# Seven block products for gate and up in both feed-forward layers, activation forms summed by accumulating DMAs, and weight loads issued by a plan of times

## The chip, the core and the metric

The kernel runs on one core of a Trainium2 chip. TensorE (PE) multiplies, with its weight loads shown as an engine of their own (PEld); VectorE (DVE), ScalarE (ACT) and GpSimd (POOL) do the element work; SyncE (SP) issues most DMAs, GpSimd some. Every engine runs its own instructions in order and waits for others by semaphores, and so does each engine that issues DMAs. The metric is the device time of one execution in microseconds (us), the median of the runs.

## The reference, cut to what matters

A decoder trunk of two layers over 512 tokens and width 1024. Layer 0 mixes by a recurrent group (RG-LRU) and a stick-breaking attention group, layer 1 by sliding-window attention (SWA); each is followed by a conv-gated MLP with 2816 inner channels. Six vectors per layer (shift, scale and gate, twice) come from `c` by one large matrix, `ada_w`.

```python
def adaln_params(c, w, b):
    m = jax.nn.silu(c) @ w + b
    return [t[:, None, :] for t in jnp.split(m, 6, axis=-1)]

def conv_ffn(h, w_gate, w_up, conv_w, conv_b, w_down):
    a = causal_dwconv(h @ w_gate, conv_w, conv_b)
    return (jax.nn.silu(a) * (h @ w_up)) @ w_down

for layer in range(DEPTH):                       # 2
    sh1, sc1, g1, sh2, sc2, g2 = adaln_params(c, ada_w[layer], ada_b[layer])
    h = rms_norm(x, norm_mix_g[layer]) * (1.0 + sc1) + sh1
    mix = ...                                    # RG-LRU + stick-breaking, or SWA
    x = x + g1 * mix
    h = rms_norm(x, norm_ffn_g[layer]) * (1.0 + sc2) + sh2
    x = x + g2 * conv_ffn(h, ...)
```

## The kernel before

**Numbers.** Every float32 operand of a large product is split in two float32r parts, hi (a copy on ACT, L200 or L169) and lo (the difference, on DVE, L201 or L170). A product is three matmuls, hi·hi, hi·lo, lo·hi (`mm3`, L209 to L212). x and h lie as [128, 8 blocks of channels, 512 tokens].

**Feed-forward, layer 0** (`ffn`, L705). For each of 22 blocks `f` of 128 inner channels, gate (`g`) and up (`u`) are each 8 x 3 = 24 matmuls with 512 columns. After groups of 8, 7 and 7 blocks the down products (`d`) of the group follow. Each weight is one load of 512 KB on SP, one hi copy and one lo difference, prepared up to three units ahead (`take`, L188).

**Feed-forward, layer 1** (`ffn_pairs`, L771). Blocks 0 and 1 are done as in layer 0. The other 20 go in ten pairs. For a pair, gate and up weights over the two halves of the channels of h make a 2 x 2 block matrix, h makes another (two halves of channels, two halves of tokens), and the product of the two takes seven block products (slots A to G) and not eight. A slot is 24 matmuls with 256 columns (`product`, L906, matmuls at L917). It needs sums of weight blocks and sums of quarters of h:
- Weights: `s1` and `s3` are loaded by SP and another block is added by an accumulating DMA that POOL issues (L868); `s2` and `s4` are added by POOL (L873, 128x1024).
- h: four forms `n1`, `n2`, `t3`, `t4`. `whole` (L805) puts hi and lo back together on POOL (L811, 8 additions of 128x512); `form` (L815) adds two of these on DVE (L819, L821, 8 operations) and splits the result (L200, L201).
- Slots run in a list `order`: A of pair i, then B, C, D of pair i-1, then E, F, G of pair i; down products after pairs 3 and 7. `upkeep` (L1003) goes ahead of each: loads for the next 9 items, weight sums for the next 4, splits for the next 4. Tile buffers: `raw` 3, `sw` 4, `adaw` 2, split weights 4.

**What goes ahead of a feed-forward.** `out_tail` (L653) ends the mixing layer; `tail` (L630) and `Norm` make h in two halves of tokens. Each of 8 blocks in a half is one DVE operation (L295), one ACT copy to `h` hi (L299) and one DVE operation to `h` lo (L301), all 128x256, while PE runs `g` and `u` of blocks 0 and 1 on what is ready.

**adaLN vectors.** 96 columns; each is a 512 KB load (`adaw`) and one DVE operation of 128x1024 (`ada_col`, L225). 16 are done at the start. `ada_step` (L229) spreads the other 80: 27 of them in the mixing of layer 0 and 53 in the feed-forward of layer 0, three after each block. None stands in layer 1.

**RG-LRU gates.** Two 64-row gate blocks per c are loaded, and split to `gwh` and `gwl` (L504), one buffer each. **SWA** (`swa_s`, L1103): 16 steps, each with sums and maxima (L1124), a reciprocal (L1130) and a scaling (L1132) on DVE, exponentials on ACT (L1128), transposes (L1145) and products on PE; `q`, `out` products go in between.

**Order.** A scheduler orders instructions for each engine by program order and priority; `pin` keeps those named in the order of the program.

## Time and profile before

| | us |
|---|---|
| median of 3 runs | 1152.72 (1151.48 to 1153.03) |
| profiled execution, its own time | 1145.14 |
| span of the profile | 1143.4 |
| PE busy | 1112.9 |
| feed-forward of layer 0, first to last PE instruction | 241.8 to 608.8 |
| feed-forward of layer 1 | 789.6 to 1139.8 |

The span runs from the first to the last instruction. Windows are in us from the span's start. A matmul's duration includes its pipeline, so matmuls overlap; what one costs in a row of many is the length of the stretch over their number.

### The profile page before, as it was taken

Reading aid. Unit: us, or ns where it says so; the run is one execution under the profiler, and the core shown is the slowest. Engines: PE = TensorE matmul, PEld = TensorE weight load, DVE = VectorE, ACT = ScalarE, POOL = GpSimd, SP = SyncE. Lnnn points to the kernel's source line nnn. Section 1 sums busy time; section 2 is a strip of 40 time slices with the busy share of each in tenths; the row PEclk is TensorE's granted clock in tenths of the full one; section 3 lists DMA queues with packets and bytes.
Section 4 is the critical chain, followed back from the end, with each engine's and each line's share of the span. In section 5 each row is a group of like instructions: output and inputs, shape, how many; then the busy total and the mean of one; then the engine's idle time right before and its main releaser. Section 6 shows DMA issues by size and latency. Waiting matters only on the chain.

```text
span 1143.4 us, 16343 instructions
## 1 busy us (share of the span) xinstructions
PE 1112.9 (97%) x6290; PEld 937.4 (82%) x6290; DVE 834.5 (73%) x1283; ACT 535.4 (47%) x864; POOL 111.2 (10%) x99
## 2 busy tenths in 40 slices
PE   8998998999999999999999999999899999999998
PEld 7866776798878888888889766678899889998997
DVE  6975899888873587456557578967999539974873
ACT  4465778354331333223335466644566326641550
POOL 0010000000000000000000111211633102411200
PEclk9999899999999999999999999999999999999999
DMA  9879573625874477445241421035358527573521
GB/s 341 297 188 234 179 213 121 199 69 168 274 225 143 135 225 236 160 148 164 81 143 57 111 57 55 19 93 143 80 136 222 158 77 198 135 236 92 132 72 74
DMA packets 49147, 174.03 MB, mean 152 GB/s; under 512 B 5583, under 2 KB 6735, under 8 KB 48367
## 3 DMA queue, kind: packets, MB, share of 16 engines
q1 hardware_dynamic: 44830, 156.64, 42.9%
q0 software_dynamic: 4240, 16.35, 7.8%
q8 instruction: 49, 0.80, 0.3%
q14 instruction: 28, 0.23, 0.1%
HBM read 164.06 MB, written 2.10 MB: 145 GB/s over the span
## 4 chain that ended last, share of the span: by engine, by line
PE 80%; DVE 9%; DMA 4%; ACT 3%; issue 2%; POOL 1%; SPq 0%; DVEq 0%; ACTq 0%; POOLq 0%
PE y L917 9%; PE d L212 7%; PE d L211 7%; PE d L210 7%; PE x L917 7%; DMA adaw<-adaw 4%; PE g L210 3%; PE g L212 3%; PE g L211 3%; PE u L212 3%; PE u L210 3%; PE u L211 3%; PE o L210 2%; PE o L212 2%; PE o L211 2%
## 5 line engine op out<-in xcount | busy, mean ns | idle before, releaser
L169 ACT ACTIVATE whi_w<-raw_w 128x1024 fp32r<-128x1024 f32 (+1 forms) x113 | 117.8, 1043 | 187.6 <-PE d L211 80.0
L170 DVE TENSOR_TENSOR wlo_w<-raw_w,whi_w 128x1024 fp32r<-128x1024 f32 (+1 forms) x113 | 135.9, 1203 | 46.0 <-ACT whi_w L169 43.5
L225 DVE CUSTOM_DVE_ANT_0 adaw<-adaw,c_s,col 128x1024 f32<-128x1024 f32 x80 | 101.3, 1279 | 35.1 <-DMA adaw<-adaw 34.9
L324 DVE SCALAR_TENSOR_TENSOR x<-d,ada,x 128x512 f32<-128x512 f32 (+1 forms) x51 | 36.6, 719 | 113.9 <-PE d L212 113.9
L211 PE MATMUL g<-h,whi_w 128*128 128x512 f32 (+1 forms) x192 | 72.2, 376 | 3.5 <-DVE h L301 3.5
L210 PE MATMUL g<-h,whi_w 128*128 128x512 f32 (+1 forms) x192 | 72.4, 377 | 1.6 <-ACT h L299 1.4
L212 PE MATMUL u<-h,wlo_w 128*128 128x512 f32 (+1 forms) x192 | 72.1, 376 | 0.0
L210 PE MATMUL d<-ah,whi_w 128*128 128x512 f32 (+1 forms) x190 | 71.9, 378 | 0.2 <-ACT ah L200 0.2
L210 PE MATMUL u<-h,whi_w 128*128 128x512 f32 (+1 forms) x192 | 72.0, 375 | 0.0
L212 PE MATMUL g<-h,wlo_w 128*128 128x512 f32 (+1 forms) x192 | 72.0, 375 | 0.0
L211 PE MATMUL d<-al,whi_w 128*128 128x512 f32 (+1 forms) x190 | 70.8, 373 | 0.8 <-DVE al L201 0.8
L211 PE MATMUL u<-h,whi_w 128*128 128x512 f32 (+1 forms) x192 | 71.5, 372 | 0.0
L212 PE MATMUL d<-ah,wlo_w 128*128 128x512 f32 (+1 forms) x190 | 71.3, 376 | 0.0
L873 POOL TENSOR_TENSOR r_s<-r_s,r_a 128x1024 f32<-128x1024 f32 x20 | 55.1, 2755 | 147.6 <-DVE wlo_s L201 50.2
L200 ACT ACTIVATE whi_s<-r_s 128x1024 fp32r<-128x1024 f32 x40 | 42.5, 1062 | 46.0 <-PE d L211 17.8
L212 PE MATMUL d<-ah,wlo_d 128*128 128x512 f32 (+1 forms) x158 | 60.8, 385 | 0.0
L210 PE MATMUL d<-ah,whi_d 128*128 128x512 f32 (+1 forms) x158 | 60.1, 380 | 0.6 <-DVE x L324 0.6
L211 PE MATMUL d<-al,whi_d 128*128 128x512 f32 (+1 forms) x158 | 60.5, 383 | 0.0
L917 PE MATMUL y<-h,whi_a 128*128 128x256 f32 x320 | 57.1, 280 | 1.0 <-DVE gt L789 1.0
L1121 POOL COPY sc<-nsink 128x4 f32<-128x4 f32 x16 | 3.4, 217 | 560.9 <-PE d L212 502.3
L917 PE MATMUL y<-forms,whi_s 128*128 128x256 f32 x320 | 56.6, 279 | 0.1
L201 DVE TENSOR_TENSOR wlo_s<-r_s,whi_s 128x1024 fp32r<-128x1024 f32 x40 | 51.9, 1297 | 5.6 <-ACT whi_s L200 4.7
(332 smaller groups left out, 3119.8 us busy)
## 6 DMA issues: line engine op xcount, KB each, us to landing
raw_w<-wu SPq DMA_DIRECT2D x104, 512.0 KB, 3.8
adaw<-adaw SPq DMA_DIRECT2D x80, 512.0 KB, 4.4
r_a<-ws SPq DMA_DIRECT2D x30, 512.0 KB, 3.8
r_s<-ws SPq DMA_DIRECT2D x20, 512.0 KB, 4.6
r_s<-ws POOLq DMA_DIRECT2D x20, 512.0 KB, 7.2
first_w<-adaw SPq DMA_DIRECT2D x16, 512.0 KB, 5.7
r_d<-wu SPq DMA_DIRECT2D x16, 512.0 KB, 5.2
raw_w<-w SPq DMA_DIRECT2D x16, 448.0 KB, 3.4
```

The source lines that it names most:

```text
L169: pin(A.activation(hi[:, :n], raw[:, :n], AF.Copy))
L170: pin(V.tensor_tensor(out=lo[:, :n], in0=raw[:, :n], in1=hi[:, :n].bitcast(F32), op=ALU.subtract))
L200: A.activation(dst_hi, src, AF.Copy)
L201: V.tensor_tensor(out=dst_lo, in0=src, in1=dst_hi.bitcast(F32), op=ALU.subtract)
L210: PE.matmul(out, whi, rhi, start=first, stop=False)
L211: PE.matmul(out, whi, rlo, start=False, stop=False)
L212: return PE.matmul(out, wlo, rhi, start=False, stop=last)
L225: return V.tensor_tensor_reduce(out=t, in0=t, in1=c_s, scale=1.0, scalar=C(f"ada_b{l}", s * 8 + m), op0=ALU.mult, op1=ALU.add, accum_out=a ...
L324: V.scalar_tensor_tensor(out=x[:, m, sl], in0=bank[:, sl], scalar=ada_ap(l, s, m), in1=x[:, m, sl], op0=ALU.mult, op1=ALU.add)
L873: G.tensor_tensor(out=self.t, in0=self.base[0].t, in1=self.base[1].t, op=ALU.add)
L917: m = [PE.matmul(out, w[a][:, o:o + P], b[c][:, k], start=slot in "AEF" and k + a + c == 0, stop=k == 3 and a == 1, skip_group_check=True) ...
L1121: nc.gpsimd.tensor_copy(sc[:, :, 256:257], nsink[:, 4 * kv:4 * kv + 4].unsqueeze(2))
```

## The change

1. **Layer 0 uses the seven block products too.** `ffn_pairs` becomes `ffn` for both layers; the old `ffn` goes. The weights of layer 0 are laid out as those of layer 1.
2. **Forms of h.** The 8 POOL additions and 8 DVE additions go. `Norm.chunk` calls `extra`: one more ACT copy of 128x256 per block and half writes the quarters of h in float32, some negated (16 copies a layer). Accumulating DMAs, issued by POOL (`add_to`, ten of 256 KB a layer), add them one after the other into the same tiles; `split_form` splits after each step.
3. **Plan of times.** Each job adds 2.8, 4.1 or 5.5 to a clock. Loads are sorted by use minus `lead` (16, 20, 24 or 26; 8 for adaLN columns) and issued in that order, pinned; `a12` has one buffer of its own. Sums stand 12 ahead of use (accumulating ones `lead` - 5).
4. **adaLN columns.** In the feed-forward of layer 0 41 stand: one in each pair from the third on, two before each down product after pairs 3 and 7, two near the end. Ten go to SWA (one every second step), one to the feed-forward of layer 1.
5. **Gates.** `gwh` and `gwl` become one tile `gw` with two buffers.

```diff
-            gwh = pers.tile([P, 256], F32R, tag="gwh", name=f"gwh{c}", bufs=1)
-            gwl = pers.tile([P, 256], F32R, tag="gwl", name=f"gwl{c}", bufs=1)
+            gw = work.tile([P, 2, 256], F32R, tag="sq", name=f"gw{c}")
+            gwh, gwl = gw[:, 0], gw[:, 1]
...
+        def extra(m, sl, t):
+            if m < 4:
+                A.activation(b["b11"][:, m], t[:, sl], AF.Identity, bias=ada_ap(l, 3, m))
+            else:
+                A.activation(b["n21"][:, m - 4], t[:, sl], AF.Identity, bias=nsh[:, l, m:m + 1], scale=-1.0)
...
+            def extra(m, sl, t):
+                if m < 4:
+                    A.activation(n12[m // 2][:, m % 2], t[:, sl], AF.Identity, bias=nsh[:, l, m:m + 1], scale=-1.0)
+                else:
+                    A.activation(b22[m // 2 - 2][:, m % 2], t[:, sl], AF.Identity, bias=ada_ap(l, 3, m))
...
-            rings = {"raw": (3, []), "sw": (4, []), "adaw": (2, []), "w": (4, [])}
+            rings = {"raw": (3, []), "a12": (1, []), "sw": (4, []), "ada": (4, []), "adaw": (2, []), "w": (4, [])}
...
-                        nc.sync.dma_start(self.t[:, :self.width], self.src)
+                        pin(nc.sync.dma_start(self.t[:, :self.width], self.src))
...
+            def add_to(a, b):
+                for i in range(2):
+                    G.dma_start(a[i], b[i], accum_op=ALU.add)
...
+            def loads(c):
+                now, full = order[c][0].at, set()
+                for it in list(to_load):
+                    if it.at - it.lead > now:
+                        break
+                    if it.t is None and (it.tag in full or not it.room()):
+                        full.add(it.tag)
+                        continue
+                    it.load()
+                    to_load.remove(it)
...
+            loads(0)
+            sums(0, 1)
+            add_to(fb, n12)
+            preps(0, pin)
+            sums(0, 2)
+            for i in ((0, 1), (2, 3)):
+                proj2([pairs[j] for j in i], HI)
...
+            split_form(n1, fb)
+            add_to(fb, b22)
+            add_to(b22, n12)
+            preps(0, pin)
+            for f in range(2):
+                finish(f, early[2 * f], early[2 * f + 1], 1.0)()
+                if f == 0:
+                    split_form(n2, fb, True)
+                    add_to(fb, fn)
...
+        if i % 2 == 0:
+            ada_step()
```

**POOL at the start of layer 1's feed-forward.** Before (`r<-h,h` are the additions of `whole`, `r_s<-ws` accumulating weight DMAs, `r_s<-r_s,r_a` weight sums):

```order
L811 TENSOR_TENSOR r_0_6819<-h_0_1880,h_1_1881 128x512
L868 DMA r_s_0_6883<-ws 128x1024
L868 DMA r_s_0_6887<-ws 128x1024
L811 TENSOR_TENSOR r_1_6821<-h_0_1880,h_1_1881 128x512
L873 TENSOR_TENSOR r_s_0_6892<-r_s_0_6883,r_a_0_6879 128x1024
L873 TENSOR_TENSOR r_s_0_6895<-r_s_0_6892,r_a_0_6881 128x1024
L868 DMA r_s_1_6945<-ws 128x1024
L811 TENSOR_TENSOR r_0_6823<-h_0_1880,h_1_1881 128x512
L811 TENSOR_TENSOR r_1_6825<-h_0_1880,h_1_1881 128x512
```

Now (`b_1` is the tile that starts as a quarter of h, `ahn`, `aln`, `ahb`, `alb`, `n_1` the other quarters):

```order
L796 DMA r_s_1_0_7839<-ws 128x1024
L801 TENSOR_TENSOR r_s_1_0_7863<-r_s_1_0_7839,r_a_1_0_7841 128x1024
L801 TENSOR_TENSOR r_s_1_0_8068<-r_s_1_0_7863,r_a_1_0_7843 128x1024
L796 DMA r_s_1_0_7845<-ws 128x1024
L796 DMA r_s_1_1_7849<-ws 128x1024
L843 DMA b_1_7403<-ahn_1_7786 128x512
L843 DMA b_1_7403<-aln_1_7787 128x512
L843 DMA b_1_7403<-ahb_1_7788 128x512
L843 DMA b_1_7403<-alb_1_7789 128x512
L843 DMA ahb_1_7788<-ahn_1_7786 128x512
L801 TENSOR_TENSOR r_s_1_1_8213<-r_s_1_1_7849,r_a_1_1_7847 128x1024
L843 DMA alb_1_7789<-aln_1_7787 128x512
```

The additions are gone from POOL; the DMAs that took their place wait in its queue among the weight sums. In layer 0's feed-forward POOL had no row before and has the like of these now, with one weight sum ahead of the first `b` row and the second between.

**DVE in the RG-LRU group of layer 0**, at the end of its first pair. Before:

```order
L170 TENSOR_TENSOR wlo_w_888<-raw_w_885,whi_w_887 128x1024
L225 ISA adaw_2_6_915,ada<-adaw_2_6_915,c_s,col 128x1024
L225 ISA ada 128x1
L526 SCALAR_TENSOR_TENSOR r_756<-a_862,r_756 128x512
L526 SCALAR_TENSOR_TENSOR r_777<-a_865,r_777 128x512
L201 TENSOR_TENSOR gwl_967<-graw_964,gwh_966 128x256
```

Now:

```order
L532 SCALAR_TENSOR_TENSOR r_759<-a_864,r_759 128x512
L532 SCALAR_TENSOR_TENSOR r_779<-a_867,r_779 128x512
L166 TENSOR_TENSOR wlo_890<-raw_887,whi_889 128x1024
L221 ISA adaw_2_6_917,ada<-adaw_2_6_917,c_s,col 128x1024
L221 ISA ada 128x1
```

The two `r` rows, for which ACT waits there, moved ahead of the adaLN column. On ACT the copies of the next gate blocks moved behind the GELU that follows.

**DVE in SWA**, at its first two steps. Before:

```order
L1130 RECIPROCAL m_0_5367<-m_0_5367 128x4
L1132 TENSOR_SCALAR sc_0_5366<-sc_0_5366,m_0_5367 128x128 x2
L1130 RECIPROCAL m_0_5392<-m_0_5392 128x4
L1124 ISA sc_1_5461,m_1_5462<-s_1_0_5451,cs,nsink,nrq_0_5131 128x256
L1124 ISA m_1_5462 128x1
L1132 TENSOR_SCALAR sc_0_5391<-sc_0_5391,m_0_5392 128x128 x2
```

Now:

```order
L1184 RECIPROCAL m_0_6432<-m_0_6432 128x4
L1186 TENSOR_SCALAR sc_0_6431<-sc_0_6431,m_0_6432 128x128 x2
L221 ISA adaw_3_5_6446,ada<-adaw_3_5_6446,c_s,col 128x1024
L221 ISA ada 128x1
L1184 RECIPROCAL m_0_6460<-m_0_6460 128x4
L1178 ISA sc_1_6529,m_1_6530<-s_1_0_6519,cs,nsink,nrq_0_6196 128x256
```

An adaLN column stands in the middle of a step; ten such stand in the stage.

## Rows read from the trace of the kernel before

**Rows 1.** The page: engines (busy us, share, instructions), and the ending chain.

```profile
PE 1112.9 (97%) x6290; PEld 937.4 (82%) x6290; DVE 834.5 (73%) x1283; ACT 535.4 (47%) x864; POOL 111.2 (10%) x99
PE 80%; DVE 9%; DMA 4%; ACT 3%; issue 2%; POOL 1%; SPq 0%; DVEq 0%; ACTq 0%; POOLq 0%
```

**Rows 2.** Waits of PE: output, line <- releaser: us, times, longest.

```profile
PE gr L210 <- ACT ge L529: 4.1, 1, 4.1
PE g L211 <- DVE h L301: 3.5, 4, 1.6
PE pr L210 <- ACT xcs L200: 2.2, 1, 2.2
...
PE d L211 <- DVE al L201: 0.8, 1, 0.8
```

**Rows 3.** Windows, layers 0, 1, 1, 1: busy per engine, clock, DMA share, GB/s.

```profile
376.90:453.80 76.90, 76.90 (x337) 63.10 (x336) 56.82 (x78) 25.91 (x34) 0.00 (x0) 1.00 0.64 207
841.80:895.50 53.70, 53.70 (x458) 53.70 (x457) 51.54 (x61) 34.31 (x47) 15.77 (x10) 1.00 0.77 204
895.50:939.50 44.00, 44.00 (x195) 36.10 (x194) 17.40 (x17) 8.55 (x9) 4.85 (x2) 1.00 0.31 99
939.50:1015.60 76.10, 76.10 (x673) 76.10 (x672) 69.80 (x84) 49.65 (x68) 22.46 (x14) 1.00 0.68 180
```

**Rows 4.** Windows at the start of the feed-forwards: layer 0, then layer 1 twice.

```profile
241.80:265.40 23.60, 23.60 (x200) 23.56 (x201) 19.42 (x40) 12.26 (x23) 0.00 (x0) 1.00 0.22 67
789.60:820.60 31.00, 27.08 (x201) 25.78 (x202) 27.56 (x43) 11.47 (x23) 19.09 (x13) 0.94 0.59 152
820.60:841.80 21.20, 19.11 (x146) 18.47 (x145) 21.20 (x27) 14.10 (x23) 9.18 (x3) 0.92 0.39 100
```

**Rows 5.** Timeline of DVE there: start, us, operation, [idle before <-releaser].

```profile
801.61 3.53 DVE L301 SCALAR_TENSOR_TENSOR h<-ht,ada,h 128x256 fp32r<-128x256 f32 x2 [0.18 <-ACT h L299]
...
807.62 0.87 DVE L301 SCALAR_TENSOR_TENSOR h<-ht,ada,h 128x256 fp32r<-128x256 f32 x2
```

**Rows 6.** Timeline of POOL in the same place.

```profile
799.91 4.94 POOL L873 TENSOR_TENSOR r_s<-r_s,r_a 128x1024 f32<-128x1024 f32 x2 [4.21 <-DMA r_s<-ws]
...
811.27 2.98 POOL L811 TENSOR_TENSOR r<-h,h 128x512 f32<-128x512 f32 x2 [1.42 <-DVE h L301]
```

**Rows 7.** Line L868, accumulating weight DMAs: issue ns min/median/max; landing.

```profile
L868 POOL DMA_DIRECT2D r_s<-ws x20: 816/874/951, 792.2 to 1075.5; - x20
...
DMA to landing us min/median/max: 5.3/7.2/9.8
```

**Rows 8.** DMA issues: SBUF to SBUF from POOL, xcount, size, median us to landing.

```profile
k<-k POOLq DMA_DIRECT2D x4, 256.0 KB, 4.7
```

**Rows 9.** The page's groups: adaLN column, weight sum: xcount | busy us, mean ns.

```profile
L225 DVE CUSTOM_DVE_ANT_0 adaw<-adaw,c_s,col 128x1024 f32<-128x1024 f32 x80 | 101.3, 1279 | 35.1 <-DMA adaw<-adaw 34.9
...
L873 POOL TENSOR_TENSOR r_s<-r_s,r_a 128x1024 f32<-128x1024 f32 x20 | 55.1, 2755 | 147.6 <-DVE wlo_s L201 50.2
```

**Rows 10.** Windows: most of SWA; layer 0, gate and up; layer 1, ten us.

```profile
675.00:755.00 80.00, 78.69 (x396) 52.87 (x395) 70.94 (x190) 55.44 (x152) 16.64 (x26) 1.00 0.14 40
265.40:331.30 65.90, 65.90 (x290) 54.11 (x289) 55.23 (x79) 25.28 (x33) 0.00 (x0) 1.00 0.75 241
882.00:892.00 10.00, 10.00 (x88) 10.00 (x87) 9.37 (x12) 7.76 (x11) 1.76 (x2) 1.00 0.97 247
```

**Rows 11.** Timeline of ACT around the first wait of rows 2.

```profile
107.45 0.42 ACT L200 ACTIVATE gwh<-graw 128x256 fp32r<-128x256 f32 x1 [4.82 <-DMA graw<-gate]
...
112.44 1.26 ACT L529 ACTIVATE ge<-gr 128x512 f32<-128x512 f32 x2 [3.27 <-DVE r L526]
```

**Rows 12.** Timeline of DVE in the same place.

```profile
110.50 1.28 DVE L225 CUSTOM_DVE_ANT_0 adaw<-adaw,c_s,col 128x1024 f32<-128x1024 f32 x1 [2.79 <-DMA adaw<-adaw]
...
111.71 1.29 DVE L526 SCALAR_TENSOR_TENSOR r<-a,r 128x512 f32<-128x512 f32 x2
```

**Rows 13.** Timeline of ACT as layer 0's h is made.

```profile
243.12 0.91 ACT L299 ACTIVATE h<-ht,ada 128x256 fp32r<-128x256 f32 x2 [1.00 <-DVE ht L295]
```

More of the change, by code (lines that the diff above doesn't have):

```diff
@@ L771, in ffn_pairs, with ffn @@
-    def ffn_pairs(l, early):
+    def ffn(l, nrm, nxt=None, before=None, after=None):
         LO, HI = HALVES
@@ new lines, in ffn @@
+            units = [unit(f"{n}{l}", i) for i in range(2) for n in ("g", "u")]
+            pairs = [(b, take(u, 2 - j, pin)) for j, (b, u) in enumerate(zip(early, units))]
+            proj2(pairs, LO)
+            b11, n21 = (nrm.forms[n] for n in ("b11", "n21"))
+            n12, b22 = act_tiles(f"n12_{l}", (P, 2, 256), F32), act_tiles(f"b22_{l}", (P, 2, 256), F32)
+            def extra(m, sl, t):
[3 more added lines that the diff above has]
+                    A.activation(b22[m // 2 - 2][:, m % 2], t[:, sl], AF.Identity, bias=ada_ap(l, 3, m))
@@ L1003, in upkeep @@
-            def upkeep(c):
-                for it, _, _ in order[c:c + 9]:
-                    if it.t is None and it.base is None:
-                        if not it.room():
-                            break
-                        it.load()
+            job(tails[1], lambda w: (down_part(2, w), down_part(3, w)), 5.5)
+            ada_item()
+            ada_item()
+            job(tails[2], down_rest, 5.5)
+            last = [Item(f"d{l}_2_{m}", w6[l * 4 + m - 4], "raw", 768) for m in range(4, KC)]
@@ new lines, in loads, with sums @@
+            def loads(c):
[8 more added lines that the diff above has]
+                    to_load.remove(it)
+            def sums(c, most=99):
+                now = order[c][0].at
+                for it in list(to_sum):
+                    if it.at - (it.lead - 5 if it.plus is not None else 12) > now or most == 0:
+                        break
+                    if not it.sums:
+                        if it.t is None and it.base is None or it.base and not (
+                                it.room() and all(b.t is not None for b in it.base)):
+                            continue
+                        it.sum()
+                        most -= 1
+                    to_sum.remove(it)
@@ L1028, in ffn_pairs @@
-            for c, (it, run, last) in enumerate(order):
-                upkeep(c)
+                        r = rings["w"][1]
+                        if it.w is None:
+                            if len(r) >= 4 and r[-4].left or it.t is None and not it.room():
+                                break
+                            it.prep(pin)
+            early_w = [Held() for _ in range(2)]
+            rings["w"][1].extend(early_w)
+            fb, fn = twos(b11), twos(n21)
+            loads(0)
@@ new lines, in ffn, with late_forms @@
+            preps(0, pin)
[4 more added lines that the diff above has]
+                    add_to(fb, fn)
+            def late_forms():
+                split_form(t3, b22)
+                split_form(t4, fb)
+            gone = []
+            for c, (it, run, done) in enumerate(order):
+                if it is blocks[0]["G"]:
+                    late_forms()
+                loads(c)
+                sums(c)
+                preps(c)
+                if it.ada is not None:
+                    with tc.high_priority(offset=-100):
+                        pin(ada_col(*it.ada, it.t))
+                    gone.append(it)
+                    continue
@@ L1030, in ffn_pairs @@
                 it.prep()
                 run(it.w)
-                if last:
+                if done:
                     it.held.left = 0
+                while gone:
+                    gone.pop().left = 0
+            if nxt is None:
+                return None
+            pending.extend(unit_order(1))
+            prep_spare([unit("l1_v", u) for u in range(2)], kept("spare1", [P, 2, 1024]))
+            for it in last[2:]:
+                it.prep()
+            prefetch(1)
+            tail(nxt, lambda m, sl, mid=None: down_last(m, last[m - 4].w, (sl,), mid), (KC - 2, KC - 1), before)
@@ L1035, in trunk @@
+            return after()
     nrm1 = Norm(1, 0)
```

363 lines of the change are left out of this document (150 added, 213 removed).

## The prediction, made before the changed kernel ran

> **What bounds the kernel now.** I read the page first: PE is busy 97% of the span and carries 80% of the chain that ended last [rows 1]. So time is taken out only where PE has less to do or waits less. Of PE's waits the largest stand in the RG-LRU group of layer 0 and at the start of layer 1's feed-forward [rows 2]. The windows show what matmuls cost. In layer 0, 376.9 to 453.8 holds 14 units of gate or up, 24 matmuls of 512 columns each: 76.9 / 14 = 5.49 us a unit, 21.97 us for the four units of a pair of blocks. In layer 1, 841.8 to 895.5 holds 19 slots of block products, 2.826 us each, and 939.5 to 1015.6 holds 28, 2.718 us each [rows 3]; PE has no gap in any of the three. Seven slots are 19.78 us at the one rate, 19.03 us at the other. So the trace already shows both ways of doing the same work, in full running.
>
> The start of the feed-forward is the other place. Layer 0 needs 23.6 us for gate and up of blocks 0 and 1 and waits for nothing. Layer 1 needs 31.0 us for the same, then 21.2 us for six slots that are worth 6 x 2.83 = 17.0 us [rows 4]: together 11.6 us too many. What I see there: two operations of DVE that make h lo take 3.53 us, 0.87 us a little later [rows 5]; over the first POOL runs its weight sums, 4.94 us for two, and it goes on with the additions of `whole` [rows 6]. PE waits for those h rows [rows 2], and its granted clock is 0.94 and 0.92 in these windows [rows 4], so after such waits it ran some us at the lower of its two levels (1.2 and 2.4 GHz), which makes the loss larger than the waits.
>
> **The change, part by part.** The sum is made against the profiled execution, 1145.14 us with a span of 1143.4 us. That execution is 7.58 us below the median of the runs; I take the difference for the median as it comes out for the profile.
>
> *Block products in layer 0.* Ten pairs of 21.97 us are 219.7 us. In layer 1 the slots ahead of the first down products ran at 2.826 us, those behind at 2.718 us, at the same granted clock of 1.00, 2.4 GHz [rows 3]; the trace does not show why. I let layer 0 do the same: 25 slots at 2.826 and 45 at 2.718 are 70.7 + 122.3 = 193.0 us. That is **-26.7 us**; -21.9 if all run at the slow rate, -29.4 if all at the fast one. All other matmuls of the feed-forward stay as many. The one wait of `d` for `al` in layer 0, 0.8 us [rows 2], goes: down products now stand three slots behind the last block they read. **-0.8 us.**
>
> *Forms, layer 1.* POOL's eight additions and DVE's eight additions go. What stays on POOL ahead of the forms is two weight sums, 2.76 us each [rows 9], which can still hold DVE up as in rows 5. I take 5 us of the 11.6 us to stay, about the two sums: **-6.6 us**, between -11.6 (nothing stays) and +1 (the chain below takes the place of the additions and is later).
>
> *Forms, layer 0.* This stage lost nothing and now gets the forms. They are a chain of three links: add a quarter, split, add the next into the same tile. A link is two issues of 0.87 us [rows 7], a landing of 4.7 us, by the nearest row, an SBUF to SBUF DMA of 256 KB [rows 8], and about 2 us of splits (two DVE operations, each of twice the size of those in rows 5, behind an ACT copy): 8.4 us; three are 25 us. What PE has in the meantime, from the time that half of the second half of h is made: some 9 us of gate and up (96 matmuls of 0.118 us, less the first few), then slots A and E (5.7 us) before F needs the first link, 2.8 us more before G needs the second, and A, B, C (8.5 us) and G before D needs the third. That is 15, 17 and 29 us against 8, 17 and 25 us. It just fits, but two weight sums of 2.76 us stand between in POOL's queue, so G may be 5 us late, behind it all of PE. I take **+3 us**; 0 if landings are quick, +12 if they take the 7.2 us of the accumulating weight loads [rows 7] in each link (3 x 2.5 us more). The extra ACT copies, 16 a layer of 0.46 us, lie in ACT's idle time between copies, 1.00 us after each two [rows 13]: nothing; without that cover half of them, 3.6 us, would come on top, which the +12 and the range allow for.
>
> The rows tell that 20 accumulating DMAs were issued in 0.82 to 0.95 us each, while DVE was busy nearly all the time [rows 7, 3], so none was held up. A rule speaks against forms by these DMAs: the Trainium skill, page "SBUF — State Buffer", section "SBUF: two separate sides", says that some DVE operations lock GpSimd out of writing descriptors, and gives about 620 ns alone against 3100 ns overlapped. By it three links would be some 7.4 us later, an estimate from that page, which is the rival of late forms, below; by the rows it is nothing, and I go by the rows.
>
> *adaLN columns.* Ten columns of 1.28 us [rows 9] come into SWA, 12.8 us on DVE. From 675 to 755 DVE is busy 70.9 of 80 us [rows 10], so 9.1 us are free and 3.7 us are over: **+4 us**, between 0 (they find the looser ends of the stage) and +12.8 (each on the path). In layer 0's pairs DVE has 51.5 / 53.7 of 19.78 = 19.0 us of work a pair ahead of the first down products, 17.5 of 19.03 us behind [rows 3]. One column more makes 20.3, over by half a microsecond for two pairs, and 18.7, not over: **+1 us**, up to +8 if each of the eight is on the path. The 32 columns at the two blocks of down products are 20.5 us in each stretch of 44 us in which DVE works 17.4 us [rows 3]: covered.
>
> *Gates of RG-LRU.* ACT waited 4.82 us for a gate load before the GELU, then 3.27 us for `r` [rows 11], and DVE had `r` behind an adaLN column whose load it waited for, 2.79 us [rows 12]. PE's waits of 4.1 and 2.2 us come from these [rows 2]. In the new order both stand ahead of what held them up. Next late is the second pair's `xc`, by the same loads. I take half: **-3 us**, between -6.3 and 0; an order by chance can cost a microsecond, too.
>
> *Plan of times for loads.* In layer 1 loads by the old rule left no gap on PE after 841.8, so there is nothing to gain. The plan keeps distances of 16 to 26 us for loads that land in 5 to 10 us even where they accumulate [rows 7]. I take 0; its risk is a rival.
>
> Sum: -26.7 - 0.8 - 6.6 + 3 + 4 + 1 - 3 = -29.1 us; span 1114.3 us; median 1152.7 - 29.1 = **1123.6 us**. With the smaller doubts the forecast's own range is 1113 to 1135 us.
>
> **Rivals.** *Late forms in both layers.* The chain takes 12 us in layer 0 (for 3) and 12 in layer 1 (for 5): 16 us more, 1139.6 us. For it: POOL works in order, each link waits for a landing, then for ACT and DVE, and PE's clock fell when it waited there [rows 4]. Against it: the cover counted above. *SWA bound by DVE:* all ten columns on the path, 8.8 us more, 1132.4 us. For it: DVE at 89% there. *DMA at the down products:* eight weights, 16 adaLN loads and the next pair's blocks are some 16.7 MB in about 60 us, 278 GB/s. A stretch of plain loads ran at 241 GB/s with the engines 0.75 busy, so 321 full; with accumulating DMAs among them they were 0.97 busy at 247 GB/s [rows 10]. At 247 the loads take 7.6 us longer at each of two places: 15 us more, 1138.6 us. *The gain is not there:* DVE, at 92 to 96% in the pairs [rows 3], sets the pace with its columns so that a pair of layer 0 takes what it took: 1150.3 us, no change by the measure below. *Slower:* SP now issues in a fixed order and `a12` has one buffer. A load that waits for that buffer holds those behind it, weights of the next pair among them. A sum is planned 12 us ahead of use, takes 2.8 us on POOL [rows 9] and about as much again for its split, so some 6 us are to spare. If each of the 20 pairs of both layers finds one weight 8 us later than planned, PE loses 2 us a pair, 40 us: 1163.6 us. It decides from 1.5 us a pair on (29.1 / 20), 7.5 us behind the plan. Against it: `a12` is freed by a sum some 14 us before the next one is used.
>
> **How the numbers follow.** A measurement of this kernel can tell about 0.2%, 2.3 us, from no change. Chances: the forecast 0.62, late forms 0.13, SWA 0.08, DMA 0.07, no gain 0.04, slower 0.06. Faster is the first four, 0.90; same 0.04; slower 0.06. The range of 8 in 10 is 1111 to 1141 us: it takes in nearly all of the forecast, SWA, and the centres of late forms and DMA, with half of what is around them, and leaves out the last two.
>
> **What would show it.** In the profile after: layer 0's feed-forward from first to last PE instruction near 344 us, not 367; its pairs 19 to 20 us apart with no gap of PE; windows at both starts with POOL at some 6 us and not 28, and PE waiting for the forms (`n`, `forms`, `h` out of the splits) under 5 us a layer; DVE above 95% in SWA with PE's waits there 4 us longer; the `gr` wait smaller. Wrong would be: waits of PE for split weights in the pairs (the plan of loads, or DVE), SP's queue waiting on `a12`, or DMA share at 0.95 and above over the down products with PE idle.

## The result: slower by 5.9%, and the profile after

The changed kernel takes 1220.2 us (median; 1218.2 to 1222.7) against 1152.8 us for the kernel before in the same comparison (1151.5 to 1153.0): ratio 1.0588, interval 1.0561 to 1.0616. The forecast was 1123.6 us, with a range of 1111 to 1141 us. The profiled execution after has a span of 1221.0 us, 77.6 us more than the one before.

The page after, engines and ending chain, as [rows 1] of before:

```profile
PE 1128.9 (92%) x7004; PEld 984.9 (81%) x7004; DVE 902.1 (74%) x1374; ACT 595.0 (49%) x973; POOL 180.7 (15%) x147
PE 50%; DMA 9%; DVE 9%; ACT 3%; issue 3%; POOL 0%; SPq 0%; ACTq 0%; DVEq 0%; POOLq 0%
```

PE's share of the chain falls from 80% to 50%. Matmuls have fewer columns on the whole now, and yet PE is busy for 16.0 us more than before: part of them ran at a lower granted clock (mean 0.962, before 0.992). The other 61.6 us of the difference PE stands still. Its waits, by total, as [rows 2]:

```profile
PE d L206 <- ACT whi_d L196: 15.7, 5, 4.4
PE y L873 <- ACT p L882: 12.4, 2, 6.2
PE g L207 <- DVE h L298: 9.4, 4, 4.9
PE x L873 <- ACT whi_a L196: 6.6, 2, 4.5
PE y L873 <- ACT whi_a L196: 5.7, 2, 3.0
PE pr L206 <- ACT xcs L196: 5.7, 1, 5.7
```

The first line is new and is what the prediction called covered: down products wait for their split weights. The second and the fifth lie in the pairs behind them. The stages, from the starts of PE's first instruction of each kind in the traces (`loads_free` and `start_t4` are experiments, below):

| us | before | after | `loads_free` | `start_t4` |
|---|---|---|---|---|
| all up to layer 0's first gate product | 241.8 | 246.9 | 246.3 | 246.3 |
| feed-forward 0, with k and v of layer 1 | 391.7 | 454.8 | 389.7 | 383.4 |
| ... of it up to the first down product | | 109.9 | 111.1 | 104.8 |
| first q product of layer 1 to its first gate product | 156.2 | 154.5 | 154.0 | 154.5 |
| feed-forward 1 up to the first down product | 105.9 | 112.5 | 112.8 | 102.4 |
| the rest, up to the end of PE's last matmul | 244.2 | 248.3 | 243.4 | 248.4 |

So 63.1 of the 77.6 us are lost in the feed-forward of layer 0, where the forecast had a gain. Windows of after, with the columns of [rows 3]: the start, the slots up to the first down product, the first block of down products, part of the slots behind it, the second block of down products, then a long run of slots in layer 1:

```profile
246.90:280.10 33.20, 26.71 (x201) 26.08 (x202) 27.06 (x41) 19.97 (x41) 11.96 (x11) 0.90 0.84 217
280.10:356.80 76.70, 72.24 (x602) 71.95 (x601) 66.47 (x85) 48.26 (x70) 21.58 (x13) 0.98 0.62 168
356.80:416.10 59.30, 49.73 (x196) 38.38 (x195) 26.71 (x39) 7.80 (x8) 0.88 (x1) 0.91 0.50 156
427.00:460.00 33.00, 23.63 (x145) 22.84 (x146) 21.86 (x20) 11.84 (x18) 14.50 (x8) 0.79 0.78 217
514.50:571.70 57.20, 49.65 (x196) 39.14 (x195) 28.14 (x40) 8.36 (x8) 0.88 (x1) 0.91 0.53 169
1012.80:1091.80 79.00, 79.00 (x673) 79.00 (x673) 67.64 (x84) 49.22 (x68) 17.84 (x10) 1.00 0.50 141
```

Eight down products took 44.0 us in [rows 3]; here they take 59.3 and 57.2 us. DVE is busy for less than half of that and the DMA engines for half, so neither is full. Behind them, at 427 to 460, PE is busy 23.6 of 33 us and its granted clock falls to 0.79.

The reason is a ring of waits, and one turn of it can be read from three queues. SP's queue in the first block of down products (start, us, operation; `r_ada` is an adaLN load, `r_d` the load of one down weight):

```profile
362.80 1.53 SPq L788 DMA_DIRECT2D r_ada<-adaw  x2
364.43 0.38 SPq L788 DMA_DIRECT2D r_d<-wu  x1
376.36 1.54 SPq L788 DMA_DIRECT2D r_ada<-adaw  x2
377.99 0.38 SPq L788 DMA_DIRECT2D r_d<-wu  x1
387.64 1.53 SPq L788 DMA_DIRECT2D r_ada<-adaw  x2
389.26 0.38 SPq L788 DMA_DIRECT2D r_d<-wu  x1
```

What ACT and then DVE do between the second and the third `r_d`, from their timelines:

```profile
384.09 1.06 ACT L196 ACTIVATE whi_d<-r_d 128x1024 fp32r<-128x1024 f32 x1 [10.22 <-DMA r_d<-wu]
```

```profile
385.18 1.23 DVE L197 TENSOR_TENSOR wlo_d<-r_d,whi_d 128x1024 fp32r<-128x1024 f32 x1 [5.42 <-ACT whi_d L196]
386.32 1.28 DVE L221 CUSTOM_DVE_ANT_0 r_ada<-r_ada,c_s,col 128x1024 f32<-128x1024 f32 x1
387.53 0.08 DVE L221 DVE_READ_ACCUMULATOR2_ANT ada<- 128x1 f32 x1
387.53 1.28 DVE L221 CUSTOM_DVE_ANT_0 r_ada<-r_ada,c_s,col 128x1024 f32<-128x1024 f32 x1
```

The weight issued at 377.99 lands, and ACT starts on it at 384.09, 6.1 us later. DVE splits it at 385.18 and only then computes two columns, since the order of the program puts `preps` ahead of the column of the same step and prepares weights of steps ahead. Each column frees one of the four `ada` tiles. For these two tiles two `r_ada` loads wait at the head of SP's queue (387.64), and behind them, in the pinned order of the plan, the next `r_d` (389.26). So one down weight comes per turn of 11.27 us, and PE needs one in 44.0 / 8 = 5.5 us [rows 3]. SP's waits for columns, over both sides of the first block of down products (340 to 430):

```profile
SPq L788 <- DVE ada L221: 76.5, 13, 18.5
```

The weights that are ahead at the start run out, then PE goes at the pace of the ring. Weights of the next pair stand behind the same loads; that is the slow stretch behind each block.

### The profile page after: what moved, and what is told of

Same layout as the page of the kernel before. It is cut to its first block, busy times and chain, and to the rows that moved or that the text cites. A ratio compares the mean times of both kernels' runs of the same rounds, so it can differ in the third digit from the quotient of the medians.

```text
span 1221.0 us, 18190 instructions
## 1 busy us (share of the span) xinstructions
PE 1128.9 (92%) x7004; PEld 984.9 (81%) x7004; DVE 902.1 (74%) x1374; ACT 595.0 (49%) x973; POOL 180.7 (15%) x147
## 4 chain that ended last, share of the span: by engine, by line
PE 50%; DMA 9%; DVE 9%; ACT 3%; issue 3%; POOL 0%; SPq 0%; ACTq 0%; DVEq 0%; POOLq 0%
PE y L873 15%; PE x L873 11%; DMA r_d<-wu 5%; PE d L207 4%; PE d L206 4%; PE d L208 4%; DMA r_s<-ws 4%; DVE r_ada L221 2%; PE o L207 1%; PE o L206 1%; PE o L208 1%; DVE sc L1178 1%; ACT whi_d L196 1%; PE ov L1213 1%; PE q L206 1%
## 5 line engine op out<-in xcount | busy, mean ns | idle before, releaser
L206 PE MATMUL d<-ah,whi_d 128*128 128x512 f32 (+1 forms) x322 | 126.4, 393 | 15.7 <-ACT whi_d L196 15.7
L873 PE MATMUL y<-forms,whi_s 128*128 128x256 f32 x640 | 123.4, 293 | 19.0 <-ACT p L882 12.4
L208 PE MATMUL d<-ah,wlo_d 128*128 128x512 f32 (+1 forms) x322 | 125.3, 389 | 1.4 <-DVE wlo_d L197 1.3
L207 PE MATMUL d<-al,whi_d 128*128 128x512 f32 (+1 forms) x322 | 125.6, 390 | 0.0
L873 PEld LDWEIGHTS y<-forms,whi_s 128*128 128x128 f32 x640 | 104.8, 200 | 20.2 <-ACT whi_a L196 12.7
L197 DVE TENSOR_TENSOR wlo_a<-r_a,whi_a 128x1024 fp32r<-128x1024 f32 x60 | 101.7, 1705 | 16.3 <-ACT whi_a L196 15.9
L873 PEld LDWEIGHTS y<-h,whi_a 128*128 128x128 f32 x640 | 100.3, 192 | 6.4 <-ACT whi_a L196 6.1
L873 PE MATMUL y<-forms,wlo_s 128*128 128x256 f32 x320 | 93.2, 291 | 0.0
L873 PE MATMUL y<-h,wlo_a 128*128 128x256 f32 x320 | 90.8, 285 | 0.7 <-DVE wlo_a L197 0.7
L196 ACT ACTIVATE whi_a<-r_a 128x1024 fp32r<-128x1024 f32 x60 | 63.2, 1057 | 53.2 <-PE y L873 30.7
```

Source lines behind the costliest of these rows:

```text
L196: pin(A.activation(dst_hi, src, AF.Copy))
L197: pin(V.tensor_tensor(out=dst_lo, in0=src, in1=dst_hi.bitcast(F32), op=ALU.subtract))
L206: PE.matmul(out, whi, rhi, start=first, stop=False)
L207: PE.matmul(out, whi, rlo, start=False, stop=False)
L208: return PE.matmul(out, wlo, rhi, start=False, stop=last)
L873: m = [PE.matmul(out, w[a][:, o:o + P], b[c][:, k], start=slot in "AEF" and k + a + c == 0, stop=k == 3 and a == 1, skip_group_check=True) ...
```

## The experiments

### The ring: three ways to open it

`cut_link` keeps every load, the order on SP and the columns' time on DVE and takes away the link between column and load. (To make room for the tile `junk` that the columns write, the adaLN loads have three tiles and not four; the values are not those of the reference.)

```diff
-                        pin(ada_col(*it.ada, it.t))
+                        pin(ada_col(*it.ada, junk, c_s))
```

> The changed kernel with one link cut in the feed-forwards: the adaLN loads go, in the same order on SP's queue and with the same bytes, into tiles that nothing reads, and the columns are computed by the same DVE instructions from the tile of c; so the adaLN values of those columns are not what the reference wants. Nothing waits any more between a column on DVE and an adaLN load on SP. Theory (a closed loop: the weight load of a down product stands on SP behind two adaLN loads, these wait for columns, and these stand on DVE behind the split of the down weights before): the two down stages of layer 0 go from 59.3 and 57.2 us back to about 44 us each, and the late weights of the pairs behind them (some 23 us of gaps) go too: 50 to 58 us, about 1165 us. Rival DMA rate at the down products: bytes and order are the same, so 1215 us or more. Rival DVE time of the columns: the same instructions, so 1215 us or more.

It took 1154.2 us; ratio to before 1.0038 (1.0006 to 1.0070). The down products of layer 0 take 44.1 us, twice. The first block of them and the slots behind, as windows:

```profile
353.10:397.20 44.10, 44.10 (x196) 36.20 (x195) 35.99 (x51) 8.67 (x9) 3.05 (x3) 1.00 0.88 310
397.20:476.20 79.00, 79.00 (x674) 79.00 (x673) 75.14 (x91) 49.41 (x68) 23.56 (x14) 1.00 0.66 200
```

PE has no gap in either. The same bytes pass at 310 GB/s with the DMA engines 0.88 busy, so DMA rate was not the limit; DVE has the same columns within 44 us, so neither was its time. From the first down product to the first q product it takes 281.4 us and after took 344.9 us: the ring cost 63.5 us, more than expected. The two stretches as windows, after and `cut_link`:

```profile
356.80:701.70 344.90, 302.56 (x1858) 271.32 (x1856) 240.93 (x327) 123.37 (x171) 44.38 (x27) 0.92 0.56 172
```

```profile
353.10:634.50 281.40, 279.42 (x1859) 256.56 (x1857) 240.34 (x327) 124.86 (x171) 41.32 (x27) 0.99 0.64 207
```

Of the 63.5 us PE stands still for 40.4 (42.3 against 2.0). In the other 23.1 us it is busy longer with the same matmuls, since its mean granted clock is 0.92 and not 0.99: over a third of the price of the ring is the clock.

`loads_free` undoes one word of the change, the pin on loads:

```diff
-                        pin(nc.sync.dma_start(self.t[:, :self.width], self.src))
+                        nc.sync.dma_start(self.t[:, :self.width], self.src)
```

> The changed kernel with one part undone: the loads of the feed-forwards are no longer held in the order of the plan, the scheduler may move them. By the program's order the weights of down products then stand on SP's queue ahead of the adaLN loads by several. Theory closed loop: the loop is open where a weight load does not stand behind an adaLN load that waits for a column, so down stages near 44 us and 1165 to 1180 us. Rival DMA rate: the same bytes in the same time, 1210 us or more. Rival DVE time of the columns: 1210 us or more.

1150.7 us; ratio 1.0026 (1.0002 to 1.0050), under the range given. The scheduler now puts the weights of the fifth to seventh down product one after another ahead of the adaLN loads that wait. SP's longest wait for a column in the same stretch is 3.9 us and not 18.5:

```profile
SPq L788 <- DVE ada L221: 23.5, 17, 3.9
```

Down products: 44.1 us, twice.

`cols_first` leaves the pin and moves columns ahead on DVE and adaLN loads back by 5 us of the plan:

```diff
-                preps(c)
                 if it.ada is not None:
-                    with tc.high_priority(offset=-100):
+                    with tc.high_priority(offset=100):
                         pin(ada_col(*it.ada, it.t))
                     gone.append(it)
+                preps(c)
+                if it.ada is not None:
                     continue
...
-  ... "ada", ada=q, lead=8)
+  ... "ada", ada=q, lead=3)
```

> The changed kernel with its work whole and two small moves in the feed-forwards: the columns go on DVE about one weight split earlier, and the plan puts adaLN loads 3 us ahead of their use and not 8, which puts each weight load of a down product ahead of one pair of adaLN loads more. Theory closed loop: the loop then holds two weights in flight and not one, so a cadence of about 11.3 / 2 = 5.7 us a down product in place of 7.3 us, down stages of 45 to 48 us, 1165 to 1180 us. Rivals DMA rate and DVE time: 1210 us or more.

1159.3 us; ratio 1.0080 (1.0045 to 1.0115). Down products: 44.1 us, twice, better than the cadence that I had reckoned for two weights in flight; 2.3 us of gaps stay behind them.

Three different edits, each of which opens the ring at another place, give 61 to 70 us back by their medians. That the ring is the cause of the slow-down is shown. But all three end where the kernel before stands: the expected gain of 29 us is still missing.

### RG-LRU and the sliding-window attention

`gates_old` gives the split gate weights a buffer of their own again:

> The changed kernel with the split gate weights of RG-LRU in one buffer of their own as before, and not in the ring of work tiles shared with the squares. Theory (the ring's other users hold the gate weights, so SP, which waits for the raw tile of the gates, comes late to the weights and columns behind it): the mixing of layer 0 is 4 to 5 us shorter, 1215 us. Rival (the new order of loads on SP does it, whatever the buffer): within 1 us of 1220 us.

```diff
-            gw = work.tile([P, 2, 256], F32R, tag="sq", name=f"gw{c}")
+            gw = fx.tile([P, 4, 256], F32R, tag="b11", name=f"gw{c}")
```

1216.5 us; ratio 1.0604 (1.0542 to 1.0666), which is not apart from after. PE's wait for `xcs` shrinks from 5.7 to 2.5 us and the one for `ge` grows from 3.8 to 4.9 us; the mixing ends 1.0 us earlier. That is less than executions differ by: `cut_link`, which has the instructions of after in the same order up to there, ends it at 243.5 us, 3.4 us earlier than after. The buffer shifts the wait; that it shortens the stage is not shown. What holds the stage up stands on DVE in after, as [rows 12] showed it before:

```profile
109.24 1.28 DVE L221 CUSTOM_DVE_ANT_0 adaw<-adaw,c_s,col 128x1024 f32<-128x1024 f32 x1 [9.08 <-DMA adaw<-adaw]
...
112.32 1.28 DVE L221 CUSTOM_DVE_ANT_0 adaw<-adaw,c_s,col 128x1024 f32<-128x1024 f32 x1 [1.79 <-DMA adaw<-adaw]
...
113.53 1.29 DVE L532 SCALAR_TENSOR_TENSOR r<-a,r 128x512 f32<-128x512 f32 x2
```

`r` did pass one column, as the order showed. Two others are still ahead of it, and their loads come later than before, for three weight loads are now ahead of them on SP. `rg_cols`, made from `start_t4` below, puts the columns behind the pair's last split:

```diff
             proj(bg[c], take(unit("l0_gr", c)))
-            ada_step(ADA_STEPS[2])
...
             split(yh[:, c], yl[:, c], ge[c])
+            ada_step(ADA_STEPS[2])
```

> The kernel of start_t4 with the adaLN columns of the two pairs of RG-LRU put behind the pair's last split and no longer between the gate branch and the recurrence. Theory (the input of the recurrence, r, stands on DVE behind two columns that wait for their loads, 9.7 us in one piece, and PE waits for the GELU that comes behind r on ACT): PE's waits for ge (3.1 us) and xcs (5.8 us) shrink by half or more, the mixing of layer 0 goes from 246.3 to 240 to 243 us, 1131 to 1134 us. Rival (the columns are then late for the values that need them, or the waits come from the chain itself): 1137 us or more.

1134.6 us; ratio 0.9853 (0.9796 to 0.9910), against 0.9879 for its parent: not apart by their intervals. In the profile the wait for `ge` is gone from the list and `xcs` is 3.3 and not 5.8 us; the mixing ends at 244.6 and not 246.3 us, half of the least that was expected. The theory holds all the same for its own group: from its first gate product (`gr`) to the first `v` product of the attention it takes 44.8 us, 52.2 in `start_t4`. From there to layer 0's first gate product it takes 112.7 us and not 108.0, with a new wait of 4.0 us for `w`, so over half of the gain is only moved.

`swa_none` leaves the ten columns of the sliding-window attention out (constants stand for their values):

```diff
-        if i % 2 == 0:
-            ada_step()
```

> The kernel of loads_free with the ten adaLN columns of the sliding-window attention of layer 1 left out, loads and all; these ten values are constants. Theory (DVE is full there, so the ten columns lengthen the stage): from the first key product to the first gate product 185.3 us becomes about 181, and the time falls by 4 us to 1146 or 1147 us. Rival (the columns find room): 185 us as before, 1150 us.

1153.2 us; ratio 1.0014 (0.9985 to 1.0042): no gain. From the first q product to the first gate product it has 154.7 us, with the columns 154.0 in `loads_free`. The 185 us in the expectation began at the first key product, which the new tail of layer 0 starts 6.6 us earlier, ahead of a wait; the stage itself had never grown. 80 us at about the same place in after and in `swa_none`:

```profile
743.30:823.30 80.00, 77.77 (x404) 53.42 (x404) 76.41 (x207) 54.77 (x153) 19.55 (x26) 1.00 0.27 87
```

```profile
680.30:760.30 80.00, 78.69 (x396) 52.89 (x396) 72.32 (x192) 55.42 (x153) 16.93 (x26) 1.00 0.14 42
```

DVE at 96% there still keeps up with PE.

### The start of the feed-forwards

In `loads_free` gate and up of blocks 0 and 1 take 32.8 us and the 25 slots behind them 78.3; at full pace these are 23.6 us [rows 4] and 25 x 2.826 = 70.7 us. Two causes could be seen. The first is on DVE and POOL, here in after, in the 23 us after the start of layer 0's feed-forward:

```profile
262.84 2.08 DVE L298 SCALAR_TENSOR_TENSOR h<-ht,ada,h 128x256 fp32r<-128x256 f32 x1
...
265.41 5.75 DVE L298 SCALAR_TENSOR_TENSOR h<-ht,ada,h 128x256 fp32r<-128x256 f32 x2
```

```profile
262.24 2.39 POOL L801 TENSOR_TENSOR r_s<-r_s,r_a 128x1024 f32<-128x1024 f32 x1 [10.08 <-DMA r_s<-ws]
...
266.82 3.66 POOL L801 TENSOR_TENSOR r_s<-r_s,r_a 128x1024 f32<-128x1024 f32 x1
```

Other operations of this kind take 0.48 us. Of the two in the last DVE row one took 5.35 us and the other 0.47. So the two that meet a weight sum take 2.08 and 5.35 us, and each ends 0.3 us after its sum. The Trainium skill, page "SBUF — State Buffer", section "SBUF: two separate sides", has it that DVE with two operands from SBUF and a GpSimd operation that reads SBUF share one port pair, and that whichever starts first keeps it for its whole instruction. The first meeting agrees with that: the sum starts 0.6 us ahead of the DVE operation. The second does not show it: by the profile the DVE operation starts 1.4 us ahead of its sum, and still ends behind it. POOL issues DMAs in these 1.4 us, and its spans are rough, so which came first stays open.

The second is the split of the last form, `t4`. It waits for its addition to land and holds up on ACT and DVE, in `loads_free`, the combination of products that PE waits for (`x<-y,p`), 6.4 us in layer 0:

```profile
293.86 0.69 DVE L853 TENSOR_TENSOR h<-b,h 128x512 fp32r<-128x512 f32 x1 [2.52 <-ACT h L848]
296.93 0.69 DVE L853 TENSOR_TENSOR h<-b,h 128x512 fp32r<-128x512 f32 x1 [2.38 <-ACT h L848]
...
298.67 0.76 DVE L888 TENSOR_TENSOR x<-y,p 128x256 f32<-128x256 f32 x2
```

Slot D needs `t4`; B and C, which are ahead of D, do not. `start_t4` puts the split later:

```diff
             def late_forms():
                 split_form(t3, b22)
-                split_form(t4, fb)
...
                 preps(c)
+                if it is blocks[0]["C"]:
+                    split_form(t4, fb)
```

> The kernel of loads_free with the split of the last form (t4) put two slots later on ACT and DVE, behind the split of weight s4, which slot C needs first. Theory: PE's gap of 6.4 us in layer 0 and 9.8 us in layer 1 is slot C waiting for a weight whose split stands behind t4's, so 2 to 4 us a layer go and slot D waits for the rest: 1142 to 1147 us. Rival (t4 itself or the sums are late, whatever the order): 1149 to 1152 us.

1137.1 us; ratio 0.9879 (0.9835 to 0.9924): 1.2% less than the kernel before, with 1 outside the interval. The slots up to the first down product take 71.7 and not 78.3 us in layer 0, 73.0 and not 82.8 us in layer 1: two to three times what I expected, since `t4` has landed by the time of slot D and PE no longer falls to its lower clock behind the gap (granted clock 1.00 in both, 0.96 and 0.94 in `loads_free`). The cause is the place of the split; which instruction waits behind it differs (`x<-y,p` in layer 0, a weight's split in layer 1, there for 8.3 us), and for layer 0 I had named the wrong one.

`start_acc` makes the first pair's two weight sums with accumulating DMAs from memory, and fixes the order of that pair's loads and additions ahead of the others (not shown):

```diff
+                    s2 = Item(f"s2_{l}_{i}", b[2], "adaw", plus=[b[3], b[0]], lead=26)
+                    s4 = Item(f"s4_{l}_{i}", b[2], "adaw", plus=[b[3], b[0], b[1]], lead=26)
```

> The kernel of loads_free with the two weight sums of the first pair of each layer taken off POOL's arithmetic: they are made by accumulating DMAs too (one load and two or three additions from memory), in a fixed order around the first additions of forms. Theory (the weight sums on POOL hold up the operations of DVE that make h lo, 2.0 and 4.3 us in place of 0.5, so PE waits 5.6 us for h in layer 0 and falls to its lower clock, and the forms follow late): gate and up of blocks 0 and 1 go from 32.8 to 25 us in layer 0 and from 30.0 to 26 in layer 1, 10 to 14 us in all, 1137 to 1141 us. Rival (the chain of accumulating DMAs and their landing is what is late): the added accumulations make it later, the slots ahead of the first down product grow by what gate and up lose, 1148 us or more.

1163.9 us; ratio 1.0111 (1.0060 to 1.0161). Both theories are right, for one part each. The two windows, gate and up and then the slots, of layer 0:

```profile
246.00:270.60 24.60, 24.59 (x201) 23.91 (x202) 16.57 (x36) 15.96 (x35) 4.37 (x5) 1.00 1.00 285
270.60:362.30 91.70, 76.69 (x601) 75.23 (x601) 73.15 (x90) 52.12 (x75) 30.99 (x24) 0.91 0.82 210
```

Without sums on POOL gate and up take 24.6 us in both layers, as the theory said. But the DMA engines are full (1.00), the weight of slot F lands late, and PE waits for it once in each layer, 13.4 us together:

```profile
PE x L879 <- ACT whi_s L196: 13.4, 2, 7.2
```

`start_both` has the edits of `start_acc` and `start_t4` together:

> The kernel of loads_free with both, the first pair's weight sums by accumulating DMAs and t4's split two slots later. Theory: the gains add up, 15 us, about 1135 us, which is under the kernel before. Rival (DMA landings bound the start): 1148 us or more.

1160.3 us; ratio 1.0097 (1.0062 to 1.0132). Of the 6.6 and 9.8 us that `start_t4` took off the slots, 3.6 and 1.9 are left (88.1 and 89.8 us, 91.7 in both layers of `start_acc`): PE still waits 7.1 and 6.3 us for the weight of slot F, which is later than `t4`. Gains do not add up where the later of two things decides.

`start_later` keeps the sums on POOL and puts one behind the second and one behind the third addition of forms, when h lo is done; additions and sums are pinned on POOL (not shown):

```diff
             add_to(fb, b22)
+            blocks[0]["G"].sum()
             add_to(b22, n12)
+            blocks[0]["C"].sum()
             preps(0, pin)
```

> The kernel of start_t4 with the additions of forms and the weight sums in a fixed order on POOL, the first pair's two weight sums behind the second addition of forms, so that they run when h lo is done. Theory (the sums on POOL hold up h lo on DVE, and nothing else in start_acc was wrong than its late accumulations): gate and up of blocks 0 and 1 take 24.6 us in both layers, as in start_acc, with slots up to the first down product at 72 to 75 us: 10 to 14 us less than start_t4, 1124 to 1128 us. Rival (the sums are then late for slots G and C, as the accumulations were in start_acc): 1137 us or more.

1139.4 us; ratio 0.9896 (0.9858 to 0.9933): no gain on `start_t4`. Gate and up take 24.6 us in both layers, and the slots grow to 78.0 and 78.4 us. One of POOL's sums now meets the split of a weight, which takes 1.2 us elsewhere:

```profile
283.29 3.45 DVE L197 TENSOR_TENSOR wlo_s<-r_s,whi_s 128x1024 fp32r<-128x1024 f32 x1
```

```profile
282.37 3.29 POOL L801 TENSOR_TENSOR r_s<-r_s,r_a 128x1024 f32<-128x1024 f32 x1
```

So PE's wait for h, the third line of its list, was worth little by itself: the forms and weights behind it set the end of this stage. From its start to the first down product it takes 102.6 us here and 104.8 in `start_t4` in layer 0, 103.0 and 102.4 in layer 1. How much of that is the landing of the additions and how much the sums was not tried.

`later_rg` has the edits of `start_later` and `rg_cols` together:

> start_later and rg_cols together. If both theories hold the gains add up: 1119 to 1124 us. If one falls: 1124 to 1134 us.

1136.8 us; ratio 0.9889 (0.9816 to 0.9962). The mixing of layer 0 ends at 241.0 us, 5.4 us earlier than in `start_later`; the total is not apart from those of `start_t4`, `start_later` and `rg_cols`. The lowest median is that of `rg_cols`, 1.5% under the kernel before.

### The kernel before, once more

`before_again` is one more execution of the kernel before:

> The kernel before once more, for a second profile. Theory (a run of matmuls of 256 columns keeps one of two distances, 113 or 118 ns, from one start to the next wait, by chance and not by the program): the two stretches of slots of layer 1 change their distance from one execution to another, and the span changes with them, by 3 us for 28 slots. Rival (the distance belongs to the place in the program): 118 ns ahead of the first down products of layer 1 and 113 ns behind, again.

1149.2 us, with a span of 1147.3 us. The same two stretches of slots in layer 1 as in [rows 3], now:

```profile
841.80:895.50 53.70, 53.70 (x454) 53.52 (x453) 51.18 (x61) 33.65 (x48) 16.03 (x10) 1.00 0.78 208
938.60:1017.50 78.90, 78.90 (x672) 78.90 (x671) 71.41 (x84) 49.00 (x68) 22.63 (x14) 1.00 0.69 179
```

28 slots took 76.1 us there, 78.9 here, from one program: the theory holds behind the first down products. Ahead of them it is the rival that holds. There the pace is the slow one again, 118 ns a matmul, and so it is over the last 18 slots or more ahead of layer 1's first down product in all 14 profiles of this case, and of layer 0's in the twelve that have slots there. So the slow pace ahead belongs to the place, and the pace behind changes with the execution. From the first down product of layer 1 to the end of PE's last matmul it takes 249.3 us here, 244.2 in the first profile.

## Why the prediction was wrong

By the sum of the prediction the span would be 1114.3 us; it was 1221.0. The 106.7 us between, by its terms:

| term | forecast | measured, and where | miss, us |
|---|---|---|---|
| columns at the down products "covered", plan of times 0 | 0 | +63.5, after against `cut_link` | 63.5 |
| forms, layer 1 | -6.6 | +6.6, up to the first down product | 13.2 |
| forms, layer 0 | 97.3 us up to the first down product | 109.9 us | 12.6 |
| RG-LRU gates | -3 | +5.1, all up to layer 0's first gate product, of it 3.7 in the group itself | 8.1 |
| pace of slots behind the first down products | 2.72 us a slot | 2.82 us; 4.7 us for 45 slots of layer 0 (the pace in `cut_link`), 4.1 us in the rest of layer 1 | 8.8 |
| columns in the attention | +4 | -1.7 | -5.7 |
| rest of layer 0, cause open, and 0.4 us at the end | | | 6.2 |

**The step that failed** is the sentence on the 32 columns at the down products. It compared totals: 20.5 us of columns beside 17.4 us of work in 44 us. The totals were right (`cut_link` has them in 44.1 us without a gap). What I left out is order. A column is not only time on DVE: it frees the tile that a load on SP waits for, and the plan had put that load, pinned, ahead of the next weight. The plan of times, which the sum put at 0, thus cost the 63.5 us. The prediction named this danger as a rival, a fixed order on SP in which a load that waits for a buffer holds those behind it, but tied it to `a12` and to the weights of pairs, gave it 40 us, and set it aside with an argument on `a12` alone. SP's waits at the down products are for columns (76.5 us in 13 waits, above); a second buffer for `a12` was not tried. The rings that matter are those whose tiles are freed by an engine that itself waits for something behind in the same queue; I should have followed each load's wait on SP to who frees it, for all six rings.

**Block products in layer 0** came as worked out at the slow pace: 79.0 us for 28 slots in `cut_link` are 19.75 us a pair against 21.97, -22.2 us for ten pairs; the prediction's bound for that was -21.9. The choice of the slow pace for 25 slots ahead was right by place, as all profiles have it there for most of them; the fast pace for 45 slots behind was the luck of one profile, as `before_again` shows.

**Forms.** The rival "late forms in both layers" came too, and more: 15.6 us in layer 0 and 18.2 in layer 1 over the 94.3 us that this stretch takes at full pace, where the rival had 12 and 12. Its mechanism was only half right. The chain of additions was as long as thought (a median of 5.3 us from issue to landing in after, 4.7 assumed; the longest 12.0). What I had not counted was that a split which waits for the chain stands in order on ACT and DVE, ahead of work for slots that do not need it: `start_t4` takes that away, and 13.6 us of the median of `loads_free` with it. The rest of these two stretches, 10.5 us in layer 0 and 8.1 in layer 1, is not taken apart. The rule from the Trainium skill that I weighed there, page "SBUF — State Buffer", section "SBUF: two separate sides", that some DVE operations lock GpSimd out of writing descriptors, does not show: the issues of the additions took 0.85 to 1.85 us, and not 3.1. (The 7.4 us that I set beside it counts one issue a link; with the two issues that my chain had, it is 14.9.) What shows is POOL's sums holding DVE. The trace has eight additions a layer, and not the ten that the description of the change gives.

**RG-LRU.** "Both stand ahead of what held them up" was true for one column of three. The reading of the order was right, the load of the next column was not looked at. The size of the miss is uncertain: from the first `gr` product to the first `v` product the group took 49.0 us before and 52.7 in after, but 47.4 in `before_again` and 50.6 in `cut_link`, with the same instructions up to there. The gain of 3 us is in none of them; `rg_cols`, with 44.8 us, shows that the columns held it.

**Attention.** A mean of 89% on DVE with 3.7 us too many was priced at 4 us; at 96% PE still did not wait more. The stage is 1.7 us shorter than before with the columns and 1.5 without them, so that is not their doing; its cause is open.

**Columns in layer 0's pairs.** The +1 us did not show: 28 slots of `cut_link` with a column in each pair have no gap of PE, with DVE at 95%. The bound of +8 for eight columns on the path was mis-summed; at 1.28 us each they are 10.2.

**What came as said.** Pairs without a gap of PE at some 19.8 us once the ring is open; of the signs of being wrong, the waits of PE for split weights came, though SP's queue waited for columns where `a12` was named. The DMA rival is refuted: 310 GB/s were to be had in `cut_link`, over the 278 that it had asked for. With ring and split mended the kernel takes 1137.1 us, inside the range of the forecast, still 13.5 us over its centre; of this 7.5 and 3.1 us lie at the two starts (104.8 and 102.4 us up to the first down product, for 97.3 and 99.3).

## What to carry to other kernels

Before loads are pinned in an order, write beside each load which instruction frees its buffer, and follow that instruction back on its own engine; if it stands behind something that a later load in the same queue feeds, there is a closed ring, and its pace is the latency of one turn (here 11.3 us), whatever the engines' totals say. The same holds for an instruction that waits for a long chain, such as a split after several additions by DMA: its place is just ahead of its first user, not where its input is made. A wait at the head of PE's list may be worth next to nothing when something behind it is as late (8.5 us less at gate and up were 2.2 us less at the first down product); what it is worth is seen only by taking it away.

## What the runs showed of the hardware that was not expected

A long row of matmuls of 256 columns keeps one of two paces at the same granted clock of 1.00: 28 slots of 24 matmuls took 76.1 us in the profile of [rows 3], 78.9 in `before_again`, 79.0 in after; that is 113 or 117.5 ns a matmul. In all 14 profiles the pace stayed the same from one late matmul to the next, where late is a start more than 130 ns after the last; it changed only there, in `start_t4` after matmuls that started 302 and 195 ns after the one before. Ahead of the first down products it was the slow one in every profile; behind them it differed between executions of one program. What sets it stays open. For the changed kernel, with 45 slots a layer behind them, it is worth up to 90 / 28 x 2.9 = 9.3 us. The profile from which I forecast had its 45 at the fast pace, `before_again` at the slow one, 5.0 us apart over that stretch: part of why it was 7.6 us below its median.
